# Feed-forward parts as units of one shape, with ScalarE and VectorE work written in a fixed order

## The chip, the cores and the metric

One Trainium2 chip; the program runs on one of its cores. The metric is the device time of the whole program in microseconds (us), the median of several executions. A TensorE matmul here takes a 128x128 block of weights and streams 128x256 or 128x512 features past it into a PSUM bank.

## The reference, cut to what matters

Two decoder layers, 512 tokens of 1024 features. Each layer runs a feed-forward half step, a token mixer (convolution and differential attention), and a second feed-forward half step:

```python
def swiglu(h, w_gate, w_up, w_down):
    return (jax.nn.silu(h @ w_gate) * (h @ w_up)) @ w_down

for l in range(DEPTH):
    x = x + 0.5 * swiglu(rms_norm(x, ffn1_norm[l]), ffn1_w_gate[l], ffn1_w_up[l], ffn1_w_down[l])
    h = rms_norm(x, mix_norm[l])
    ...                                             # the mixer
    x = x + jnp.concatenate([conv_out, diff_out], axis=-1) @ w_out[l]
    x = x + 0.5 * swiglu(rms_norm(x, ffn2_norm[l]), ffn2_w_gate[l], ffn2_w_up[l], ffn2_w_down[l])
```

The hidden width is 2816, which is 22 tiles of 128. Everything is float32. There are four feed-forwards in the program (two layers, two each); they are what the change touches.

## The kernel before, in words

**Numbers as pairs.** Weights and features are split into a high part (`whi`, `hh`, `acth`, `th`) and a low part (`wlo`, `hl`, `actl`, `tl`) that TensorE can multiply in its fast float32 form. A product is the sum of three matmuls: high by high, high by low, low by high. ScalarE makes the high part (a copy, `parts_of`, L100), VectorE the low part (raw minus high, L101).

**Parts.** `PARTS` (L45) cuts the 22 hidden tiles of a feed-forward into 5, 8 and 9. The first part of 5 is computed plainly. The parts of 8 and of 9 use a seven-product scheme (Winograd's form of Strassen's) in place of eight products of half blocks. A part first computes its hidden tiles, one gate and up tile at a time ("gate-up", `sums` L135 and `seven` L369), and then its share of the output projection in four steps, two output tiles a step ("down", `down_sums` L413 and `seven_down` L468). So the second part has 8 gate-up steps and 4 down steps, the third 9 and 4.

**One gate-up step.** `sums` loads the weights: the gate block g1,g2 (L145), then a tile with g1 and u2 (L147, L148), u2 once more (L150); then a DMA on GpSimd's queue adds u1 onto both halves of that second tile (L152, an accumulating transfer), which leaves g1+u1 and u2+u1. GpSimd adds up two more sums (L157, L158). `seven` issues the products in this order, 12 matmuls of 256 columns each: `u2u1` into c, `u2` into d, then (call of `before`, L393) the rest of the step ahead, its product `g1u1` into its own a; then `g1` into a, `g2` into b, `all` into c, `g1u2u1` into a. a and d are the halves of one PSUM bank, b and c of another. ScalarE saves intermediate sums in `keep` (L391, L395, L399), VectorE adds (L400) and ScalarE applies silu (L401). The rest: L404 to L408, then `Gated.add` (L540), which splits the hidden tile `us`, still in PSUM, into `hh` and `hl` (L549, L550).

**Pairs.** The first four hidden tiles of a part are paired for the down steps. An even one is saved in `hold` and differenced (L545, L546). After the odd one come the sums of the pair, straight on in `add` (L554 to L562); they end with `four`, made from the odd tile's `us` in PSUM on ScalarE (L561) and VectorE (L562).

**PSUM banks.** `pair_banks` (L325) gives each step two banks and goes around three such pairs. A step takes over the banks of the step three before it, and TensorE's first write waits until everything that reads the old contents is done.

**Weights in SBUF.** `ring` (L92) hands out buffers: five for raw weights (`wraw`), four each for high and low parts. A load waits until the old buffer has been read.

**What sets the order.** A scheduler with a model of the instructions' times orders each engine's queue when the program is built. `tc.keep_in_program_order` fixes one instruction behind the one traced before it on its engine. In the kernel before, only the first matmul of each product is fixed so; ScalarE, VectorE and GpSimd stand as the scheduler put them. Each engine then runs its queue strictly in order.

## Time and profile before

| | |
|---|---|
| median of 3 runs | 1799.3 us (1799.25 to 1803.62) |
| the profiled execution | 1802.17 us |
| its span, first to last instruction | 1800.2 us |
| TensorE granted clock | 0.999 |
| busy: VectorE, ScalarE, GpSimd | 1343.9, 977.6, 884.8 us |

The profile is one execution. PE is TensorE's matmuls, PEld its weight loads, DVE VectorE, ACT ScalarE, POOL GpSimd, SP the engine that issues most DMAs. `out<-in` names the program's tiles. A line such as L100 is a line of the kernel. An engine's idle time is put down to the instruction that released it.

### The profile page before, as it was taken

Reading aid. Unit: us, or ns where it says so; the run is one execution under the profiler, and the core shown is the slowest. Engines: PE = TensorE matmul, PEld = TensorE weight load, DVE = VectorE, ACT = ScalarE, POOL = GpSimd, SP = SyncE. Lnnn points to the kernel's source line nnn. Section 1 sums busy time; section 2 is a strip of 40 time slices with the busy share of each in tenths; the row PEclk is TensorE's granted clock in tenths of the full one; section 3 lists DMA queues with packets and bytes.
Section 4 is the critical chain, followed back from the end, with each engine's and each line's share of the span. In section 5 each row is a group of like instructions: output and inputs, shape, how many; then the busy total and the mean of one; then the engine's idle time right before and its main releaser. Section 6 shows DMA issues by size and latency. Waiting matters only on the chain. (4 is left out here: it accounts for less than half of the span.)

```text
span 1800.2 us, 30317 instructions
## 1 busy us (share of the span) xinstructions
PE 1776.3 (99%) x11437; PEld 1609.4 (89%) x11437; DVE 1343.9 (75%) x2021; ACT 977.6 (54%) x1691; POOL 884.8 (49%) x661
## 2 busy tenths in 40 slices
PE   9999999999999999999999999999999999999999
PEld 7899999888788899899888998998877888999998
DVE  7877687768857868687776776878688587786874
ACT  6465465545844456466543654655457454564652
POOL 2244545669952134444612354356699521345443
PEclk9999999999999999999999999999999999999999
DMA  7374565433122365565433645744331223655752
GB/s 245 109 186 123 146 180 148 139 107 94 47 71 82 94 164 130 141 181 151 127 118 98 165 117 156 185 135 154 93 99 43 71 94 88 167 145 146 181 148 71
DMA packets 112307, 231.36 MB, mean 129 GB/s; under 512 B 12215, under 2 KB 33990, under 8 KB 112160
## 3 DMA queue, kind: packets, MB, share of 16 engines
q1 hardware_dynamic: 92064, 191.93, 33.2%
q0 software_dynamic: 19808, 37.33, 12.2%
q8 instruction: 89, 1.46, 0.3%
q14 instruction: 58, 0.48, 0.1%
q10 hardware_dynamic: 288, 0.16, 0.0%
HBM read 227.26 MB, written 3.42 MB: 128 GB/s over the span
## 5 line engine op out<-in xcount | busy, mean ns | idle before, releaser
L100 ACT ACTIVATE whi<-wraw 128x512 fp32r<-128x512 f32 (+3 forms) x660 | 496.0, 777 | 498.1 <-PE ps_pair L386 135.5
L101 DVE TENSOR_TENSOR wlo<-wraw,whi 128x512 fp32r<-128x512 f32 (+2 forms) x617 | 602.7, 1000 | 179.2 <-ACT whi L100 174.2
L386 PE MATMUL ps_pair<-acth,wlo 128*128 128x256 f32 x1088 | 308.3, 283 | 1.9 <-DVE wlo L101 1.9
L386 PE MATMUL ps_pair<-actl,whi 128*128 128x256 f32 x1088 | 307.9, 283 | 0.0
L386 PE MATMUL ps_pair<-acth,whi 128*128 128x256 f32 x1088 | 307.8, 283 | 0.0
L157 POOL TENSOR_TENSOR wraw<-wraw 128x512 f32<-128x512 f32 x68 | 104.7, 1540 | 309.0 <-DMA wraw<-in_gu 205.5
L386 PE MATMUL ps_pair<-th,whi 128*128 128x256 f32 x816 | 231.7, 284 | 4.8 <-ACT keep L395 3.7
L386 PE MATMUL ps_pair<-th,wlo 128*128 128x256 f32 x816 | 230.9, 283 | 0.0
L386 PE MATMUL ps_pair<-tl,whi 128*128 128x256 f32 x816 | 230.9, 283 | 0.0
L152 POOL DMA_DIRECT2D wraw<-in_gu x68 | 82.0, 1206 | 268.2 <-DVE gs L617 111.9
L386 PEld LDWEIGHTS ps_pair<-acth,wlo 128*128 128x128 f32 x1088 | 208.8, 192 | 2.7 <-DVE wlo L101 2.7
L386 PEld LDWEIGHTS ps_pair<-actl,whi 128*128 128x128 f32 x1088 | 208.8, 192 | 0.3
L386 PEld LDWEIGHTS ps_pair<-acth,whi 128*128 128x128 f32 x1088 | 208.8, 192 | 0.3
L177 PE MATMUL ps_pair<-actl,whi 128*128 128x512 f32 x448 | 174.7, 391 | 0.6 <-DVE actl L263 0.6
L174 PE MATMUL ps_pair<-acth,whi 128*128 128x512 f32 x448 | 173.9, 392 | 0.8 <-ACT whi L100 0.7
L178 PE MATMUL ps_pair<-acth,wlo 128*128 128x512 f32 x448 | 174.2, 390 | 0.0
L386 PEld LDWEIGHTS ps_pair<-th,whi 128*128 128x128 f32 x816 | 156.6, 192 | 6.2 <-ACT keep L395 4.7
L386 PEld LDWEIGHTS ps_pair<-tl,whi 128*128 128x128 f32 x816 | 156.6, 192 | 0.0
L386 PEld LDWEIGHTS ps_pair<-th,wlo 128*128 128x128 f32 x816 | 156.6, 192 | 0.0
L101 POOL TENSOR_TENSOR wlo<-wraw,whi 128x1024 fp32r<-128x1024 f32 x44 | 105.5, 2402 | 37.3 <-ACT whi L100 37.3
L861 DVE SCALAR_TENSOR_TENSOR ps_y<-u,par,ps_y 128x512 f32<-128x512 f32 x156 | 117.6, 754 | 3.7
L158 POOL TENSOR_TENSOR wraw<-wraw 128x512 f32<-128x512 f32 x68 | 116.1, 1707 | 5.3
(214 smaller groups left out, 4177.5 us busy)
## 6 DMA issues: line engine op xcount, KB each, us to landing
wraw<-in_gu SPq DMA_DIRECT2D x208, 256.0 KB, 4.1
wraw<-in_gu SPq DMA_DIRECT2D x104, 512.0 KB, 3.7
wraw<-in_gu POOLq DMA_DIRECT2D x68, 512.0 KB, 5.6
wraw<-in_wqkv SPq DMA_DIRECT2D x24, 512.0 KB, 3.7
wraw<-in_wag SPq DMA_DIRECT2D x16, 512.0 KB, 3.6
wraw<-in_wout SPq DMA_DIRECT2D x16, 512.0 KB, 3.6
wraw<-in_dn SPq DMA_DIRECT2D x60, 128.0 KB, 3.3
wraw<-in_dn SPq DMA_DIRECT2D x20, 384.0 KB, 3.7
```

Source lines behind the costliest of these rows:

```text
L100: S.activation(hi, raw, AF.Copy)
L101: low = (eng or V).tensor_tensor(out=lo, in0=raw, in1=f32(hi), op=ALU.subtract)
L152: nc.gpsimd.dma_start(two.rearrange("p (b c) -> p b c", b=2), u[:, h[0]].unsqueeze(1).broadcast_to([P, 2, 512]), accum_op=ALU.add)
L157: G.tensor_tensor(more[:, h[0]], two[:, h[1]], whole[:, h[0]], op=ALU.add)
L158: G.tensor_tensor(more[:, h[1]], more[:, h[0]], whole[:, h[1]], op=ALU.add)
L174: first = T.matmul(ps, wh, xh, start=start, stop=False)
L177: T.matmul(ps, wh, xl, start=False, stop=False)
L178: T.matmul(ps, wl, xh, start=False, stop=stop)
L386: mm = T.matmul(ps, l, r, start=first and i == j == 0, stop=False, skip_group_check=True)
L861: V.scalar_tensor_tensor(ys[c] if t == PAD and not n else y, us[c][:, t : t + SEQ], pars[l][:, wc + t : wc + t + 1], y, op0=ALU.mult, op1= ...
```

## The change

`seven`, `down_sums` and `seven_down` become two classes, `GateUp` and `Down`, with one common `body`. The parts of 8 and 9 of a feed-forward become one list of 25 units (8 gate-up, 4 down, 9 gate-up, 4 down). The body of a unit issues its own products and, at fixed places between them, the splitting of the **next** unit's weights (`nxt.hi`, `nxt.lo`), the rest and finish of the unit ahead (`prev`), and the pair sums of the unit before that (`prev2.extras`). Every one of these ScalarE and VectorE instructions is now fixed in program order (`pinned`).

- Weights are grouped by when they are used: A holds u2u1 and u2, B holds g1 and g2, C holds g1u2u1 and all, D holds g1u1. The gate-up unit loads the tile that is added to first, then the gate block. The accumulating transfer and GpSimd's two sums stay.
- The pair sums move from `add`, one unit after the odd tile, to `combine`, called two units after it, behind the splitting of the next unit's A and D.
- In a down unit the two additions to `x` on GpSimd (L501, L510) go. VectorE adds the saved sums in PSUM and then adds to `x`: five VectorE instructions in place of three. For all but the first down unit of a part the plain products into the spare bank move ahead of the rest of the unit before.
- The product list, its order within a unit and the number of matmuls are the same.

The core of the diff (lines of the new kernel are named "new L..." below):

```diff
+    def pinned(ins, pin=PIN):
+        if pin:
+            tc.keep_in_program_order(ins)
+        return ins
...
+        def body(self, nxt, prev, prev2):
+            if nxt:
+                nxt.load()
+            self.begin()
+            self.go(self.c, "u2u1", "t1", first=True)
+            pinned(S.activation(self.keep[:, 3], self.c, AF.Copy))
+            if nxt and nxt.soon:
+                nxt.hi("A")
+                nxt.lo("A")
+            self.go(self.d, "u2", "t4", first=True)
+            self.early()
+            if nxt and self.early_free:
+                nxt.hi("B")
+            if prev:
+                prev.rest()
+            self.go(self.a, "g1", "b11")
+            pinned(S.activation(self.keep[:, :2], by_two(self.banks[0]), AF.Copy))
+            if prev:
+                prev.finish(0)
+            if nxt and self.early_free:
+                nxt.lo("B")
+            if prev:
+                prev.finish(1)
+            if nxt:
+                if not nxt.soon:
+                    nxt.hi("A")
+                    nxt.lo("A")
+                nxt.hi("D")
+                nxt.lo("D")
+            if prev:
+                prev.finish(2)
+            self.go(self.b, "g2", "b21")
+            self.middle()
+            if nxt:
+                nxt.hi("C")
+            if prev2:
+                prev2.extras()
+            self.go(self.c, "all", "b22")
+            self.go(self.a, "g1u2u1", "t2")
+            pinned(S.activation(self.keep[:, 2], self.a, AF.Copy))
+            self.close()
+            if nxt:
+                nxt.lo("C")
+                if not self.early_free:
+                    nxt.hi("B")
+                    nxt.lo("B")
...
+    class GateUp(Unit):
+        steps = KT // 2
+        soon = False
...
+        def load(self):
+            h = slice(0, 512), slice(512, 1024)
+            gate, up = self.src
+            two, g, u2 = ring("wraw"), ring("wraw"), ring("wraw2", 512)
+            nc.sync.dma_start(two[:, h[0]], gate[:, h[0]])
+            nc.sync.dma_start(two[:, h[1]], up[:, h[1]])
+            nc.sync.dma_start(g, gate)
+            nc.sync.dma_start(u2, up[:, h[1]])
+            nc.gpsimd.dma_start(
+                by_two(two), up[:, h[0]].unsqueeze(1).broadcast_to([P, 2, 512]), accum_op=ALU.add
+            )
+            more = ring("wraw")
+            G.tensor_tensor(more[:, h[0]], two[:, h[1]], g[:, h[0]], op=ALU.add)
+            G.tensor_tensor(more[:, h[1]], more[:, h[0]], g[:, h[1]], op=ALU.add)
+            self.raw = {"A": (two[:, h[1]], u2), "B": (g,), "C": (more,), "D": (two[:, h[0]],)}
...
+        def close(self):
+            g, two = self.keep[:, 0::2], by_two(self.banks[1])
+            pinned(V.tensor_tensor(two, two, g, op=ALU.add))
+            pinned(S.activation(g, two, AF.Silu))
+        def rest(self):
+            a, d, keep, us = self.a, self.d, self.keep, by_two(self.banks[0])
+            self.go(a, "g1u1", "t3")
+            pinned(V.tensor_tensor(d, a, keep[:, 3], op=ALU.add))
+            pinned(V.tensor_tensor(a, a, keep[:, 1], op=ALU.add))
+            pinned(V.scalar_tensor_tensor(us, us, -1.0, keep[:, 0::2], op0=ALU.mult, op1=ALU.mult))
+        def finish(self, n):
+            self.gated.add(self.n, self.banks[0], n)
+        def extras(self):
+            self.gated.combine(self.n, self.banks[0])
...
+    class Down(Unit):
...
+        def close(self):
+            A, B = 2 * self.q, 2 * self.q + 1
+            two, keep = by_two(self.banks[1]), self.keep
+            if not self.early_free:
+                self.plain(self.banks[1], 0)
+            pinned(V.tensor_tensor(two, two, keep[:, 0::2], op=ALU.add))
+            self.into(A, two, 0.5)
+            self.after(A)
+            if not self.early_free:
+                self.spare()
+            two = by_two(self.ps)
+            pinned(V.tensor_tensor(two, two, keep[:, 1::2], op=ALU.subtract))
+            self.into(B, two, 0.5)
...
+        def add(self, n, us, step):
+            a, b = slice(0, HS), slice(HS, SEQ)
+            first = self.paired(n) and n % 2 == 0
+            if step == 0:
+                if first:
+                    self.held[n] = self.fp.tile([P, SEQ], F32, tag=("hh8", "hl8")[n // 2 % 2], name="hold")
+                    pinned(S.activation(self.held[n], us, AF.Copy))
+                else:
+                    self.part_hi(n, us)
+            if step == 1:
+                if first:
+                    pinned(V.tensor_tensor(us[:, b], self.held[n][:, a], self.held[n][:, b], op=ALU.subtract))
+                    self.part_hi(n, us)
+                else:
+                    self.part_lo(us)
+            if step == 2 and first:
+                self.part_lo(us)
...
+        def combine(self, n, us):
+            if not self.paired(n) or n % 2 == 0:
                 return
-            t = self.hold
...
+            a, b = slice(0, HS), slice(HS, SEQ)
+            t = self.held[n - 1]
+            pinned(V.tensor_tensor(t[:, b], us[:, b], t[:, b], op=ALU.subtract))
+            pinned(V.scalar_tensor_tensor(t[:, a], t[:, a], -1.0, t[:, b], op0=ALU.mult, op1=ALU.subtract))
+            pinned(V.scalar_tensor_tensor(us[:, a], us[:, a], -1.0, t[:, a], op0=ALU.mult, op1=ALU.subtract))
             hi, lo, four = (self.part(tag) for tag in self.STORE[n // 2])
...
+            pinned(S.activation(hi, t, AF.Copy))
+            pinned(S.activation(four[:, a], us[:, a], AF.Copy))
+            pinned(V.tensor_tensor(lo, t, f32(hi), op=ALU.subtract))
+            pinned(V.tensor_tensor(four[:, b], us[:, a], f32(four[:, a]), op=ALU.subtract))
             self.sums.append((hi, lo, four))
```

In the new kernel's lines, the five pair sums on VectorE are new L668, L669, L670, L674 and L675, the two on ScalarE new L672 and L673; the three adds of the rest are new L511 to L513; the two matmul lines of the units are one, new L377.

## The prediction

> **What bounds the kernel now.** I read the page first, then the chain that ended last, then what TensorE waited for.

> ```profile
> span 1800.2 us, 30317 instructions
> ...
> PE 1776.3 (99%) x11437; PEld 1609.4 (89%) x11437; DVE 1343.9 (75%) x2021; ACT 977.6 (54%) x1691; POOL 884.8 (49%) x661
> ```

> ```profile
> 1660.75 86.43 PE ps_pair L386 x720
> ...
> 1775.98 3.43 PE ps_pair L491 x15
> ...
> 1795.46 0.70 DVE x L516
> ...
> 1796.29 0.69 DVE x L520
> ```

> In the last feed-forward 720 matmuls of 256 columns follow each other in 86.43 us, 0.120 us each; one of 512 columns takes 3.43/15 = 0.229. TensorE is the bound, and the change leaves every matmul in place. So it can only win back what TensorE waits. These are the waits of its weight loads that belong to the changed lines:

> ```profile
> PEld ps_pair L386 <- ACT keep L395: 4.7, 5, 1.4
> PEld ps_pair L491 <- DVE hl L550: 3.1, 4, 0.9
> PEld ps_pair L482 <- ACT keep L496: 3.0, 6, 1.0
> PEld ps_pair L386 <- DVE wlo L101: 2.7, 4, 1.2
> ...
> PEld ps_pair L491 <- ACT hh L549: 2.2, 1, 2.2
> ...
> PEld ps_pair L386 <- ACT keep L399: 1.3, 1, 1.3
> ```

> Together 4.7 + 3.1 + 3.0 + 2.7 + 2.2 + 1.3 = **17.0 us**: the most that can be gained, about 0.9%. Everything else that the change shortens or lengthens counts only if TensorE comes to wait for it.

> **The change, part by part.** A gate-up unit is 84 matmuls, 10.08 us; I count from its first matmul. Products take 1.44 us each: u2u1 from 0, u2 from 1.44, the rest of the unit ahead from 2.88 to 4.32, then g1, g2, all, and g1u2u1 to 10.08. Units are named by their hidden tile, 0 to 7 or 8.

> *The waits that go: -17.0.* In the new order the save of a and d (new L406) stands first in ScalarE's queue once TensorE has made them, at 5.96, 2.7 us ahead of its use; c's save is always at the unit's beginning; the last tile's hh and hl, by the sums below, are some 0.6 us early for the plain products. I take all 17.0 as gained, and half of it as the lower end.

> *The pair sums: the new wait.* They move behind the next unit's weights, and they are the last readers of a PSUM bank. In the changed program's queue the first matmul of `u2` in the units of tiles 4 and 6 waits for new L675, the last sum of the pairs 0,1 and 2,3, because those units take over the banks of tiles 1 and 3. All eight parts have both. Before, the same sums stood here (VectorE in the unit of tile 3, third part of the first feed-forward; TensorE's row is the u2 product of tile 4):

> ```profile
> 240.12 0.43 DVE L405 TENSOR_TENSOR ps_pair<-ps_pair,keep 128x256 f32<-128x256 f32 x1
> 240.59 0.43 DVE L406 TENSOR_TENSOR ps_pair<-ps_pair,keep 128x256 f32<-128x256 f32 x1
> 241.18 1.23 DVE L101 TENSOR_TENSOR wlo<-wraw,whi 128x1024 fp32r<-128x1024 f32 x1 [0.15 <-ACT whi L100]
> 242.32 0.69 DVE L408 SCALAR_TENSOR_TENSOR ps_pair<-ps_pair,keep 128x512 f32<-128x512 f32 x1
> ...
> 245.87 0.68 DVE L550 TENSOR_TENSOR hl<-ps_pair,hh 128x512 fp32r<-128x512 f32 x1
> 246.47 0.41 DVE L555 TENSOR_TENSOR hold<-ps_pair,hold 128x256 f32<-128x256 f32 x1
> 246.91 0.42 DVE L556 SCALAR_TENSOR_TENSOR hold<-hold 128x256 f32<-128x256 f32 x1
> 247.25 0.68 DVE L101 TENSOR_TENSOR wlo<-wraw,whi 128x512 fp32r<-128x512 f32 x1
> 247.85 0.42 DVE L557 SCALAR_TENSOR_TENSOR ps_pair<-ps_pair,hold 128x256 f32<-128x256 f32 x1
> 248.19 0.68 DVE L101 TENSOR_TENSOR wlo<-wraw,whi 128x512 fp32r<-128x512 f32 x1
> 248.78 0.69 DVE L400 TENSOR_TENSOR ps_pair<-ps_pair,keep 128x512 f32<-128x512 f32 x1
> 249.39 0.68 DVE L560 TENSOR_TENSOR hs<-hold,hs 128x512 fp32r<-128x512 f32 x1
> 249.99 0.42 DVE L562 TENSOR_TENSOR hs<-ps_pair,hs 128x256 fp32r<-128x256 f32 x1
> ```

> ```profile
> 257.20 0.28 PE L386 MATMUL ps_pair<-th,whi 128*128 128x256 f32 x1
> ```

> L562 ends at 250.41, and u2 starts at 257.20: 6.8 us to spare. The starts also give the pace: a queue of 512-wide instructions advances 0.60 each, a dependent 256-wide one 0.45. ScalarE's paces:

> ```profile
> 236.43 0.60 ACT L549 ACTIVATE hh<-ps_pair 128x512 fp32r<-128x512 f32 x1 [1.48 <-DVE ps_pair L546]
> 236.93 1.14 ACT L100 ACTIVATE whi<-wraw 128x512 fp32r<-128x512 f32 x2
> 237.97 0.37 ACT L399 ACTIVATE keep<-ps_pair 128x256 f32<-128x256 f32 x1
> ```

> Now VectorE's new queue in the unit of tile 3. The rest of tile 2 ends at 4.32, its last matmul drains 0.16 later. L511 4.52, L512 4.99, L513 5.46 to 6.14; low part of B to 7.29; the difference for tile 2 (new L646) to 7.63. ScalarE needs that for hh, 0.60 to 8.25, and only then splits A: first half done 8.79. VectorE: A 8.80 to 10.08, D to 10.68, hl to 11.28, then L668 to 11.60, L669 to 12.06, L670 to 12.52. ScalarE's copy L672 (0.63) ends at 12.71, L673 at 13.05; L674 runs 12.73 to 13.41, **L675 ends at 13.8**. TensorE wants that bank at 10.08 + 1.44 = 11.52: it waits **2.3 us**. Behind the waiting matmul stands all of TensorE's queue, so this is time of the kernel.

> In the unit of tile 5 no even tile is finished: A's split starts at 7.2, D ends at 9.7, L670 at 10.9, L674 at 11.83, L675 at 12.2: a wait of **0.7 us**.

> GpSimd can lengthen this. Median and longest of L560 (now L674), and GpSimd's pace:

> ```profile
> L560 DVE TENSOR_TENSOR hs<-hold,hs x16: 681/684/1802, 122.5 to 1709.6; 128x512 fp32r<-128x512 f32 x16
> ```

> ```profile
> 259.08 0.43 SPq L148 DMA_DIRECT2D wraw<-in_gu  x1
> ```

> ```profile
> 254.56 1.19 POOL L152 DMA_DIRECT2D wraw<-in_gu  x1
> 260.52 1.28 POOL L157 TENSOR_TENSOR wraw<-wraw 128x512 f32<-128x512 f32 x1 [4.77 <-DMA wraw<-in_gu]
> 261.88 2.17 POOL L158 TENSOR_TENSOR wraw<-wraw 128x512 f32<-128x512 f32 x1
> 264.56 1.20 POOL L152 DMA_DIRECT2D wraw<-in_gu  x1 [0.51 <-DMA wraw<-in_gu]
> ```

> The buffer for the tile that is added to, two tiles on, comes free with the low part of D, at 9.7 in the unit of tile 2. From there: some 0.8 to issue both pieces, 264.56 - 259.08 = 5.5 until the accumulating transfer can be issued, 260.52 - 254.56 = 6.0 until GpSimd's first sum: 9.7 + 12.3 = 22.0, or 11.9 in the unit of tile 3. So the two sums (3.5 us) cover 11.9 to 15.4, where L674 stands. I take the long L674 there, 1.1 more: 3.4. In the unit of tile 5 L674 starts before the sums: 0.7. Ends: without any lengthening 2.3 + 0.7; with L669 held up too and L674 long at tile 5 as well, 4.0 + 1.8. Eight parts: **8 x (3.4 + 0.7) = +32.8**, between 24.0 and 46.4.

> [...]

> *keep behind the sums.* The save of a (new L429) stands behind L672 and L673 and ends at about 13.4; the rest that needs it would start at 12.96. The bank wait covers it; without that, it costs 0.4 a part.

> *Ends of a feed-forward: +4.2.* TensorE's last row:

> ```profile
> 1795.85 0.28 PE L482 MATMUL ps_pair<-hs,wlo 128*128 128x256 f32 x1
> ```

> The last down unit's rest now follows directly on the product whose sum ScalarE must save first (0.16 + 0.37 + latency): 0.6 at three of four ends; at the other, matmuls of the next stage stand between. At the kernel's end five VectorE instructions follow the save, 0.62 to 4.0, while the last matmul drains at 1.5: 2.5 behind it, against 0.85 before (L520 ends at 1796.29 + 0.69 = 1796.98, the last matmul at 1795.85 + 0.28 = 1796.13): +1.6. Ahead of a mixer the same lateness reaches the statistics: I take 0.4 twice.

> *What lies beside other work.*

> ```profile
> L501 POOL TENSOR_TENSOR x<-x,keep 128x512 f32<-128x512 f32 x32 | 52.3, 1633 | 18.9 <-ACT keep L500 18.8
> ```

> GpSimd loses its 64 additions to x; VectorE gets 64 of 0.69, 44 us in the down units. There it has about 7.2 us of work (five of 0.69, and four low parts) in 10.5 or 11.9: hidden. One split in six fewer per gate-up unit also lies off the path. The accumulating loads are due at about 7.2 in the unit after that where they land at 1.8: 5 us to spare, so load order costs nothing.

> Sum: -17.0 + 32.8 + 4.2 = **+20.0**. Against the profiled execution's 1802.2 that is 1822; that execution lies 2.9 above the median of the runs, so against 1799.3: **1819.3**. This forecast alone spans 1808 to 1834.

> **The rivals.**
> - *Faster.* The fixed order removes the 17.0 and the bank comes free in time: 1799.3 - 17.0 + 4.2 = 1786.5. It decides at 7.2 us from the end of tile 2's rest (4.32) to L675; I count 9.5. For it: 6.8 us to spare before. Against it: ScalarE's and VectorE's steps in that stretch stand in one chain. [...] 0.10.
> - *No change.* Both waits together come to 1.6 a part, if VectorE starts the sums earlier than I count: 12.8 - 17.0 + 4.2 = 0, so 1799.3. 0.08.
> - *The order fits no better:* as many waits appear at other places as go: 1799.3 + 32.8 + 4.2 = 1836. Fixed queues with splits that wait on loads speak for it, the spare times above against. 0.12.
> - *The accumulating transfers set the pace:* if they land over 5 us later than in the rows above, every gate-up unit grows; at 0.5 us for each of 68, 34 more: 1853. 0.05.

> **How the numbers follow.** The forecast has 0.65. The range 1800 to 1838 leaves out the first, the last and about half of the second rival. A measurement of this kernel tells about 0.3% (5.4 us) from no change. Faster: 0.11; within: 0.08; slower: 0.81.

> **What would show it.** Right: TensorE waits for VectorE new L675 16 times, 2.3 to 4 us at tile 4 and 0.7 to 1.8 at tile 6 of each part, some 33 us in all; the old six waits are gone; VectorE's sums stand behind the low part of D; GpSimd's sums lie over L674. Wrong: no wait on L675, or waits on high and low parts of weights, or GpSimd's idle time before L472 growing in each unit.

## The result and the profile after

The changed kernel is slower: median 1856.2 us of 4 runs (1852.93 to 1859.08) against 1801.5 of 4 runs of the kernel before on the same chip; ratio 1.0303, 95% interval 1.0276 to 1.0329. The forecast was 1819.3, in a range of 1800 to 1838: the sign was right, the size was not. The profiled execution took 1854.8 us.

The page and the row of the core, after (span; busy time and share of each engine; the core's span and mean granted clock of TensorE):

```profile
span 1852.9 us, 30039 instructions
...
PE 1791.8 (97%) x11437; PEld 1621.6 (88%) x11437; DVE 1333.2 (72%) x2017; ACT 951.8 (51%) x1623; POOL 756.5 (41%) x597
```

```profile
core 0: 1852.9 us, clock 0.989
```

TensorE has the same 11437 matmuls. Its busy share fell from 99% to 97%, and its clock from 0.999 to 0.989. So two things are to be found: where it waits, and why its clock is lower. What TensorE waited for, after (total, times, longest):

```profile
PE ps_pair L377 <- DVE hs L675: 31.6, 16, 3.5
PE ps_d L138 <- ACT hh L628: 8.9, 3, 7.1
PE ps_pair L377 <- ACT keep L429: 3.2, 3, 1.4
PE ps_pair L377 <- ACT keep L406: 2.4, 2, 1.2
```

None of the six waits that the prediction added up to 17.0 us is left at its place; ScalarE's saves are waited for at the ends of a feed-forward alone (L406, L429). In their place stand 16 waits for the last pair sum, as forecast, and three rows that are not in the sum, or in it with another size.

**The pair sums.** VectorE in the unit of tile 3, third part of the first feed-forward (start, duration), GpSimd's two weight sums beside it, then TensorE at the first u2 product of tile 4:

```profile
265.89 0.69 DVE L491 TENSOR_TENSOR wlo<-wraw,whi 128x512 fp32r<-128x512 f32 x1
266.49 0.69 DVE L661 TENSOR_TENSOR hl<-ps_pair,hh 128x512 fp32r<-128x512 f32 x1
267.09 0.42 DVE L668 TENSOR_TENSOR hold<-ps_pair,hold 128x256 f32<-128x256 f32 x1
267.54 1.33 DVE L669 SCALAR_TENSOR_TENSOR hold<-hold 128x256 f32<-128x256 f32 x1
268.91 0.43 DVE L670 SCALAR_TENSOR_TENSOR ps_pair<-ps_pair,hold 128x256 f32<-128x256 f32 x1
269.57 0.98 DVE L674 TENSOR_TENSOR hs<-hold,hs 128x512 fp32r<-128x512 f32 x1 [0.23 <-ACT hs L672]
270.47 0.41 DVE L675 TENSOR_TENSOR hs<-ps_pair,hs 128x256 fp32r<-128x256 f32 x1
```

```profile
267.34 1.25 POOL L472 TENSOR_TENSOR wraw<-wraw 128x512 f32<-128x512 f32 x1 [4.48 <-DMA wraw<-in_gu]
268.67 1.33 POOL L473 TENSOR_TENSOR wraw<-wraw 128x512 f32<-128x512 f32 x1
```

```profile
270.94 0.39 PE L377 MATMUL ps_pair<-th,whi 128*128 128x256 f32 x1 [3.46 <-DVE hs L675]
...
272.20 0.42 PE L377 MATMUL ps_pair<-th,whi 128*128 128x256 f32 x1
272.42 0.42 PE L377 MATMUL ps_pair<-tl,whi 128*128 128x256 f32 x1
```

The chain is the forecast's: the low part of D (L491), hl, then the sums, and TensorE starts when L675 has ended. From the starts of the matmuls, the eight stalls at tile 4 are 2.74 to 3.61 us, at tile 6 0.80 to 1.91; in all 34.2 us beyond the normal pace, where the sum had 32.8. The last rows show something else: 1.3 us after TensorE resumes, matmuls of 256 columns start every 0.22 us instead of every 0.12. The windows of one microsecond around it (the first number after the five engines' counts is the granted clock):

```profile
268.00:269.00 1.00, 0.00 (x0) 0.00 (x0) 0.97 (x2) 0.09 (x1) 0.92 (x2) 1.00 0.76 213
...
272.00:273.00 1.00, 1.00 (x7) 1.00 (x6) 0.61 (x1) 1.00 (x3) 0.34 (x1) 0.50 0.00 0
273.00:274.00 1.00, 1.00 (x7) 1.00 (x6) 0.00 (x0) 0.34 (x1) 0.00 (x0) 0.50 0.84 121
274.00:275.00 1.00, 1.00 (x7) 1.00 (x7) 0.00 (x0) 0.00 (x0) 0.00 (x0) 0.50 1.21 197
275.00:276.00 1.00, 1.00 (x8) 1.00 (x8) 0.39 (x1) 0.00 (x0) 0.00 (x0) 0.80 0.92 154
```

For 3.4 us the clock is 0.50, and by the starts of the matmuls this costs 1.5 us. Over the span the clock is under 1 in nine stretches. TensorE stood idle in parts of them; what the matmuls in them lost adds up, by their starts, to 14.5 us, against 1.6 in the kernel before. Each stretch lies in or behind a gap of TensorE's. So a stall of 3 us can cost 3 + 1.5.

**The plain part.** ScalarE in the first feed-forward, then TensorE:

```profile
53.52 1.36 ACT L715 ACTIVATE gs<-gs 128x512 f32<-128x512 f32 x2
69.97 0.63 ACT L487 ACTIVATE whi<-wraw 128x512 fp32r<-128x512 f32 x1 [15.08 <-DMA wraw<-in_gu]
70.50 1.04 ACT L101 ACTIVATE whi<-wraw 128x1024 fp32r<-128x1024 f32 x1
71.45 0.61 ACT L628 ACTIVATE hh<-gs 128x512 fp32r<-128x512 f32 x1
```

```profile
72.11 1.22 PE L138 MATMUL ps_d<-hh,whi 128*128 128x512 f32 x2 [7.13 <-ACT hh L628]
```

L487 is the split of group D of the first of the 25 units, which come *after* the plain part. The change leaves the splits of `units[0]` to the scheduler, which put this one ahead of work that was ready. ScalarE sits 15.1 us in front of it until the accumulating transfer has landed; the plain part's hh is behind it in the queue, though it could have run: in e13 below, where this split stands later, ScalarE makes the same hh at 58.66. With two smaller places TensorE loses 9.6 us.

**The ends.** ScalarE at the end of a feed-forward that a mixer follows:

```profile
368.51 1.06 ACT L101 ACTIVATE whi<-wraw 128x1024 fp32r<-128x1024 f32 x1 [4.37 <-issue]
369.48 0.71 ACT L226 ACTIVATE acth<-x,par 128x512 fp32r<-128x512 f32 x1
370.09 0.61 ACT L235 ACTIVATE sq<-x 128x512 f32<-128x512 f32 x1
370.61 0.58 ACT L406 ACTIVATE keep<-ps_pair 128x512 f32<-128x512 f32 x1
```

The save L406 stands behind what `after` puts on ScalarE for the mixer. TensorE loses 1.36 us for it and 1.51 for L429 just after, at two ends, and 0.63 for L429 at the kernel's end: 6.4 us.

The spans differ by 52.7 us. To add up the parts, the six old waits have to be counted like the new ones, by the starts of the matmuls: so counted they come to 15.2 us. The 17.0 is idle time of the weight loads, part of which lies beside running matmuls. The sum: -15.2 + 34.2 + 9.6 + 6.4 + (14.5 - 1.6) = 47.9. Of the rest 1.7 lies at the kernel's end, where the span now goes on for 6.0 us after the start of the last matmul in place of 4.3, and some 3 in the mixers.

### The profile page after: what moved, and what is told of

It is laid out like the page before. It is cut to its first block, busy times and chain, and to the rows that moved or that the text cites. A ratio compares the mean times of both kernels' runs of the same rounds, so it can differ in the third digit from the quotient of the medians.

```text
span 1852.9 us, 30039 instructions
## 1 busy us (share of the span) xinstructions
PE 1791.8 (97%) x11437; PEld 1621.6 (88%) x11437; DVE 1333.2 (72%) x2017; ACT 951.8 (51%) x1623; POOL 756.5 (41%) x597
## 5 line engine op out<-in xcount | busy, mean ns | idle before, releaser
L491 DVE TENSOR_TENSOR wlo<-wraw,whi 128x512 fp32r<-128x512 f32 (+1 forms) x340 | 325.6, 989 | 59.2 <-ACT whi L487 59.0
L377 PE MATMUL ps_pair<-acth,whi 128*128 128x256 f32 x1088 | 308.4, 283 | 0.0
L377 PE MATMUL ps_pair<-actl,whi 128*128 128x256 f32 x1088 | 308.2, 283 | 0.0
L377 PE MATMUL ps_pair<-acth,wlo 128*128 128x256 f32 x1088 | 308.0, 283 | 0.0
L487 ACT ACTIVATE whi<-wraw 128x512 fp32r<-128x512 f32 (+1 forms) x340 | 251.0, 799 | 54.0 <-DMA wraw<-in_gu 30.4
L377 PE MATMUL ps_pair<-th,whi 128*128 128x256 f32 x816 | 235.6, 289 | 31.6 <-DVE hs L675 31.6
L472 POOL TENSOR_TENSOR wraw<-wraw 128x512 f32<-128x512 f32 x68 | 95.1, 1398 | 390.9 <-DMA wraw<-in_gu 246.0
L377 PE MATMUL ps_pair<-th,wlo 128*128 128x256 f32 x816 | 234.2, 287 | 0.0
L377 PE MATMUL ps_pair<-tl,whi 128*128 128x256 f32 x816 | 234.1, 287 | 0.0
L377 PEld LDWEIGHTS ps_pair<-acth,whi 128*128 128x128 f32 x1088 | 209.4, 192 | 0.2
L377 PEld LDWEIGHTS ps_pair<-actl,whi 128*128 128x128 f32 x1088 | 209.2, 192 | 0.2
L377 PEld LDWEIGHTS ps_pair<-acth,wlo 128*128 128x128 f32 x1088 | 209.1, 192 | 0.0
L101 ACT ACTIVATE whi<-wraw 128x1024 fp32r<-128x1024 f32 (+3 forms) x124 | 122.6, 999 | 143.3 <-PE ps_pair L141 83.3
L377 PEld LDWEIGHTS ps_pair<-th,whi 128*128 128x128 f32 x816 | 159.3, 195 | 34.9 <-DVE hs L675 34.9
L138 PE MATMUL ps_pair<-acth,whi 128*128 128x512 f32 x448 | 174.0, 395 | 0.3 <-ACT whi L101 0.2
L406 ACT ACTIVATE keep<-ps_pair 128x512 f32<-128x512 f32 x100 | 59.6, 596 | 197.3 <-PE ps_pair L377 197.3
L377 PEld LDWEIGHTS ps_pair<-th,wlo 128*128 128x128 f32 x816 | 159.8, 196 | 0.0
L377 PEld LDWEIGHTS ps_pair<-tl,whi 128*128 128x128 f32 x816 | 159.6, 196 | 0.0
L367 DVE TENSOR_TENSOR wlo<-wraw,whi 128x1024 fp32r<-128x1024 f32 (+2 forms) x128 | 123.6, 990 | 16.5 <-ACT whi L363 16.4
```

What stands on the lines that cost most here:

```text
L101: S.activation(hi, raw, AF.Copy)
L138: first = T.matmul(ps, wh, xh, start=start, stop=False)
L367: pinned(V.tensor_tensor(out=lo[:, :c], in0=self.raw[k][:, :c], in1=f32(hi[:, :c]), op=ALU.subtract), pin)
L377: mm = T.matmul(ps, l, r, start=first and i == n == 0, stop=False, skip_group_check=True)
L406: pinned(S.activation(self.keep[:, :2], by_two(self.banks[0]), AF.Copy))
L472: G.tensor_tensor(more[:, h[0]], two[:, h[1]], g[:, h[0]], op=ALU.add)
```

## The experiments

Theory 1: the place of the pair sums in VectorE's queue costs most of it, with half clock behind the stalls. Theory 2: the first unit's split in front of the plain part. Theory 3: the ends. Rivals: the fixed order as such, or the accumulating transfers. All ratios are to the kernel before on the same chip:

| kernel | median us | ratio, 95% interval |
|---|---|---|
| the change | 1856.2 | 1.0303 (1.0276 to 1.0329) |
| e1 sums early | 1818.0 | 1.0110 (1.0084 to 1.0136) |
| e2 first unit fixed | 1853.5 | 1.0306 (1.0279 to 1.0333) |
| e3 = e1 + e2 | 1812.2 | 1.0073 (1.0051 to 1.0096) |
| e4 no fixed order | 1809.6 | 1.0061 (1.0039 to 1.0083) |
| e5 = e3 + ends | 1805.5 | 1.0033 (1.0020 to 1.0046) |
| e6 = e5, D last | 1824.8 | 1.0134 (1.0120 to 1.0149) |
| e7 low D behind sums | 1842.0 | 1.0231 (1.0212 to 1.0251) |
| e8 idle matmuls | 1847.6 | 1.0266 (1.0251 to 1.0281) |
| e9 = e5, first D late, spare cut | 1817.1 | 1.0081 (1.0060 to 1.0103) |
| e10 = e9, B first | 1816.0 | 1.0073 (1.0052 to 1.0094) |
| e11 = e2, first D late | 1853.9 | 1.0285 (1.0260 to 1.0309) |
| e12 = e5, only D fixed | 1801.3 | 0.9998 (0.9983 to 1.0013) |
| e13 = change, only D fixed | 1843.1 | 1.0230 (1.0207 to 1.0253) |

**e1: the sums early.**

```diff
             pinned(S.activation(self.keep[:, 3], self.c, AF.Copy))
+            if prev2:
+                prev2.extras()
...
                 nxt.hi("C")
-            if prev2:
-                prev2.extras()
```

> The changed kernel with one call moved: the pair sums of the tile before last (L668 to L675) stand right behind the copy of c into the keep tile (L395), ahead of the additions of the unit before (L511 to L513), no longer behind the next unit's splits. Theory 1 (place of the pair sums in VectorE's queue): the 16 waits of ps_pair L377 for hs L675 (31.6 us by the chain of waits, 34.2 us by the pitch of the matmuls) go, and with them the about 8 us of matmuls at a longer pitch right behind them; 1856 becomes 1810 to 1824. Rival A (the fixed order itself holds VectorE back): what is taken out in one place comes back as waits for L511 to L513 or for keep L406 in the same units, time above 1840. Rival B (accumulating transfers set the pace): no change, 1850 to 1860. If the longer pitch has nothing to do with the stalls, 1822 and the pitch stays.

From 1.0303 to 1.0110: about 35 us came back with one moved call. The waits that take their place are small:

```profile
PE ps_d L138 <- ACT hh L628: 9.6, 4, 7.4
PE ps_pair L377 <- DVE wlo L491: 4.0, 8, 1.3
PE ps_pair L377 <- ACT keep L429: 3.2, 3, 1.4
```

No row for L675 is left, so VectorE had the time earlier in the unit. Rivals A and B fall. The gain is at the weak end of the range, since 4.0 us for low parts and 2.4 for high parts (at the unit behind the sums) are new: VectorE is nearly full in these units (busy for 0.86 of 805 to 816 us in this trace, a stretch with the sums in it).

**e2: the first unit's splits fixed too.**

```diff
-                units[0].hi(k, False)
-                units[0].lo(k, False)
+                units[0].hi(k)
+                units[0].lo(k)
```

> The changed kernel with only the splits of the first unit of each feed-forward part sequence put under the fixed order as well (the two False arguments at units[0] taken away). On ScalarE that moves one copy in each of four places: the 128x512 split of g1u1 (whi from wraw), which stood ahead of the plain part's hh copy and sat up to 15.1 us for its transfer. Theory 2: the wait of ps_d L138 for hh L628 (8.9 us in 3) goes and with it the matmuls at half pace behind it; 1856 becomes 1843 to 1847. Rival: the plain part is held by its own transfers, or the first unit is now late by the same time; 1852 to 1858. The pair sums' waits (31.6 us in 16) stay in both.

A miss: the wait for hh went and the time stayed. TensorE's waits, and VectorE ahead of the first unit's product:

```profile
PE ps_pair L377 <- DVE hs L675: 30.7, 16, 3.7
PE ps_pair L377 <- DVE wlo L491: 5.0, 6, 1.1
```

```profile
90.58 0.69 DVE L734 SCALAR_TENSOR_TENSOR x<-ps_d,x 128x512 f32<-128x512 f32 x1 [2.25 <-PE ps_d L142]
91.19 2.42 DVE L491 TENSOR_TENSOR wlo<-wraw,whi 128x512 fp32r<-128x512 f32 x3
```

Fixing all four groups put A, which the first product needs, behind the plain part's last addition to x (L734), which needs TensorE's last plain matmul. TensorE waits 1.31 us beyond its pace at the first unit of each of the four feed-forwards, 5.2 us, and 2.4 more in four waits two units on. By the starts of the matmuls 7.7 of the 9.6 us are given back, and the 2 that are left are less than the interval of the ratio. So the rival holds, the first unit is now late. That leaves Theory 2 open; e13 moves group D alone.

**e3: both.**

> Both edits: the pair sums right behind the copy of c, and the first unit's splits under the fixed order. If the two losses are separate places on one path the gains add: 42 + 12 us off 1856, so 1797 to 1808; what is left against the kernel before (1801) is then the ends of the feed-forward (about 6 us more) against the old waits that went (17 us). Rival: the two share an aftermath or another engine closes the gap: above 1815.

1812, at 1.0073: beyond the forecast 1797 to 1808. Both halves give less than was priced: the sums 35 in place of 42 (e1), and the first unit some 7 over e1 in place of 12.

**e4: no fixed order** (`PIN = False`).

> The changed kernel with the switch of the fixed order off: units, their one shape, the additions on VectorE and the accumulating transfers stay, but the scheduler orders ScalarE and VectorE. If the loss is where the fixed order puts the pair sums (Theory 1), the scheduler issues them when they are ready and most of the 16 waits go: 1800 to 1822. If the loss is the units' shape or the transfers whatever the order, 1840 to 1860.

1.0061. With units, their shape, additions on VectorE and accumulating transfers all kept, 44 us of the 55 are gone when the scheduler places the instructions. The scheduler's L675 costs no wait. Of what is left its waits show

```profile
PE ps_d L138 <- ACT hh L628: 8.9, 3, 7.1
PE ps_d L138 <- DVE x L734: 4.6, 3, 2.1
PE ps_pair L377 <- ACT keep L429: 3.2, 3, 1.4
```

**e7: a smaller dose.** Only VectorE's part of group D moves behind the sums.

```diff
                 nxt.hi("D")
-                nxt.lo("D")
...
             if prev2:
                 prev2.extras()
+            if nxt:
+                nxt.lo("D")
```

> The changed kernel with one split moved: VectorE's part of group D (one 128x512, about 0.6 us) stands behind the pair sums, no longer ahead of them. A dose test of Theory 1: if each bank wait is the length of VectorE's queue ahead of L675, every one of the 16 shrinks by that 0.6 us, about 9.5 us in all (31.6 to 22), and half a window or more of half clock with it; 1856 becomes 1842 to 1848. Rival (the waits are set by ScalarE's copies L672 and L673 or by the wait for L641, not by the queue): the 16 waits stay at 30 to 32 us and the time at 1853 to 1858.

```profile
PE ps_pair L377 <- DVE hs L676: 19.3, 10, 2.8
```

(L675 and L676 here are L674 and L675 of the change.) The waits shrink by 12.3 us, more than 9.5, and the time by some 13 (ratio 1.0303 to 1.0231). At tile 4 the stalls are 0.62 us shorter in the mean, about the length of the split that moved. At tile 6 they shrink by 0.89, as the sum ahead of the last one also runs undisturbed there more often (it takes over 1 us in one of eight, in the change in five); six of the eight fall under what counts as a wait. So the wait is the length of VectorE's queue ahead of the last sum, with what GpSimd adds to it.

**e8: TensorE kept busy in the stall.** Ahead of u2 in the unit of tile 4:

```diff
+        def fill(self):
+            if self.n == 4:
+                ps = bank("tp", "ps_idle")
+                for _ in range(10):
+                    mm = T.matmul(ps, ones_r, ones_r.unsqueeze(1).broadcast_to([P, NT, P]), start=True, stop=True)
+                    tc.keep_in_program_order(mm)
```

> The changed kernel with ten matmuls on constants (128x512, 2.27 us at full pace, into a bank of their own that nothing reads) put ahead of the first u2 matmul of tile 4, where TensorE stands 2.7 to 3.6 us for hs L675. They take nothing out of the wait for L675, but TensorE no longer idles through it. If the half clock (0.50 for 3.4 us) behind these waits comes from TensorE's standing idle, four of the windows in the trace of the changed kernel (at 271, 831, 1186 and 1746 us) go, 1.7 us each: 1856 becomes 1847 to 1851. If it comes from something else (power, transfers), they stay: 1854 to 1859.

Eight times 2.27 us of work on constants is added, and the kernel is some 7 us faster. The intervals of the two ratios touch, but the mean clocks of the runs do not: 0.993 to 0.995 in four runs, 0.987 to 0.990 in four of the change. The wait for the last sum (L686 here) is as long, only filled: 18.2 us are matmuls on constants and 14.1 stay idle, most of it at tile 6, which gets no filling. The waits and the clock:

```profile
PE ps_pair L377 <- DVE hs L686: 14.1, 16, 1.6
```

```profile
core 0: 1846.5 us, clock 0.995
```

No half clock is left behind the stalls at tile 4, where there were four, nor at tile 6, where there was one; what is left lies at the other places (plain part, attention, an end ahead of a mixer, the kernel's end), in part shorter. Transfers and pair sums are as before, so the half clock comes from TensorE's standing idle. The filling was worth about 7 us.

**e5: the ends.** The call of `after` for the second tile moves behind the saves; the last unit's plain product runs between g1u2u1 and g1u1.

```diff
+            if prev:
+                prev.done()
+            if self.last:
+                self.spare()
             self.close()
...
             self.into(B, self.a.unsqueeze(1).broadcast_to([P, 2, HS]), -0.5)
-            self.after(B)
+        def done(self):
+            self.after(2 * self.q + 1)
```

> The kernel of e3 with the end of each feed-forward rearranged: the call of after for the second tile of the unit before stands behind the copies of the keep tile, no longer ahead of them on ScalarE, and the last unit's plain product of its second tile (ps_d) runs between g1u2u1 and g1u1, where TensorE waited for keep L429. Theory 3: the waits for keep L408 (2.4 us in 2) and keep L429 (3.2 us in 3) go, and with them the two windows of half clock (1.7 us each) that stand right behind them in the trace of e3; 1812 becomes 1802 to 1806. Rival: the mixer's first work, for which the call prepares, is late by as much; 1810 to 1813.

From 1.0073 to 1.0033, about 7 us, as Theory 3 has it. The waits for the saves L406 (L408 in e3) and L429 are gone; 3.7 us in 3 for c's save (L395) took their place, and the half clock at the ends went.

**e6: D last.**

> The kernel of e5 with the next unit's g1u1 split (group D, needed last) put behind all other work of the unit on both engines, so that VectorE has the pair sums of two units and the splits that are needed at the next unit's start off its queue sooner. In e3 TensorE still waits 6.6 us in 13 for wlo L491 at the start of units; if VectorE's queue is what makes these late, they go: 1797 to 1801. Rival: they wait for the transfers or for ScalarE's halves, no change, 1802 to 1806.

A miss of the sign: 1.0134, some 18 us slower than e5. The waits for low parts grew (9.0 in 22, from 6.6 in 13), those for high parts to 5.2 in 10 (from 1.3 in 2) and those for L395 to 5.2 in 3 (from 3.7); 4.1 us in 3 for the low parts of the down weights came up. By the starts of the matmuls these make 15 of the 17 us between the two spans.

**e9 and e10.** In e9 the first unit's group D goes behind the second's A, and the last unit's plain product is cut in two; e10 moves the sums behind ScalarE's copy of B.

> The kernel of e5 with two more edits: the first unit's g1u1 split (group D, first needed by the second unit) stands behind the second unit's group A on ScalarE and VectorE, since in e5 TensorE waits 1.31 us for wlo at the second unit of each of the four part sequences (5.2 us); and the last unit's plain product is cut, two tiles early and three between g1u2u1 and g1u1, since in e5 TensorE waits 3.7 us in 3 for keep L395 there. If these waits stand on the path: 1805 becomes 1795 to 1799, level with the kernel before or a little under it (1800). Rival (VectorE's queue is full and the waits come up a unit later): 1802 to 1805.

> The kernel of e9 with the pair sums behind ScalarE's copy of group B, so that L672 and L673, which wait for VectorE, no longer hold that copy back. If ScalarE's queue makes the 0.3 to 0.4 us waits for wlo and whi at tiles 4 and 6 (about 4 us in all in e5): 2 to 4 us under e9. Rival: VectorE is the fuller one there, no change within 1 us.

Both miss: e9 is some 9 us slower than e5, e10 like e9 within the intervals. I had misread the place: the 1.31 us stand at the first unit, not the second (see e2). GpSimd's first weight sums behind 100 us, in e5 and then in e9:

```profile
104.17 1.28 POOL L480 TENSOR_TENSOR wraw<-wraw 128x512 f32<-128x512 f32 x1 [4.48 <-issue]
105.53 1.28 POOL L481 TENSOR_TENSOR wraw<-wraw 128x512 f32<-128x512 f32 x1
```

```profile
108.83 1.29 POOL L483 TENSOR_TENSOR wraw<-wraw 128x512 f32<-128x512 f32 x1 [8.27 <-DMA wraw<-in_gu]
110.19 1.63 POOL L484 TENSOR_TENSOR wraw<-wraw 128x512 f32<-128x512 f32 x1
```

Groups A and D are halves of one raw tile. Holding D's split back keeps that tile, and GpSimd's weight sums come 4.7 us later. ScalarE waits for them, and TensorE 9.2 us in 5 for ScalarE's high parts. The same may be behind e6's loss; no run shows that. The cut plain product did take away the 3.7 us for L395, and 4.5 us for the mixer's statistics (ps_rows, waiting for ssum) appeared.

**e11: e2 with the first unit's D late.**

> The changed kernel with the first unit's splits under the fixed order, as in e2, and with that unit's group D behind the second unit's group A. In e2 the wait of ps_d L138 for hh L628 (8.9 us) went and the time stayed, with 5.0 us of new waits for wlo L491, four of 1.31 us at the second units. If what e2 took away came back as these waits and as half-clock windows at other places: now 5 us less than e2 by the waits, 1845 to 1850. Rival (the plain part's stall was hidden by something else that ends as late): 1852 to 1857, as e2.

1.0285: like e2, and the four waits at the first units are still there, for the same misreading.

**e12 and e13: only group D fixed.**

```diff
-                units[0].hi(k, False)
-                units[0].lo(k, False)
+                units[0].hi(k, k == "D")
+                units[0].lo(k, k == "D")
```

> The changed kernel with only group D of the first unit's splits under the fixed order; A, B and C stay with the scheduler. If the wait of ps_d L138 for hh L628 (8.9 us in 3 by the chain of waits, and two windows of half clock behind it) stands on the path by itself: 1856 becomes 1843 to 1848, with no wait for wlo L491 in its place. Rival (what this stall takes is given back at the next waits for L675 whatever the splits' order): 1852 to 1857.

> The kernel of e5 (pair sums early, ends rearranged) with only group D of the first unit's splits under the fixed order and A, B and C left to the scheduler, as in the changed kernel. If the four waits of 1.31 us for wlo at the first units come from A standing behind the plain part's additions to x (L734 of the changed kernel), they go: 1805 becomes 1798 to 1802, level with the kernel before. Rival (VectorE is late there whatever the order): 1804 to 1807.

Both come out as forecast. In e13 the waits for hh are gone, the two longest rows are the change's others, and nothing stands in for hh:

```profile
PE ps_pair L377 <- DVE hs L675: 31.0, 16, 3.6
PE ps_pair L377 <- ACT keep L429: 3.2, 3, 1.4
```

and the ratio falls from 1.0303 to 1.0230, 13 us: Theory 2 holds after all; e2 had given the gain back at the first units. In e12, with the sums early and the ends mended, the kernel is level with the one before. Its span is 1798.6 us, its clock 1.000, TensorE is busy 99% again, and its longest rows of waits are:

```profile
PE ps_pair L377 <- DVE wlo L499: 3.8, 8, 1.3
PE ps_pair L377 <- ACT keep L395: 3.7, 3, 1.3
```

In parts of the time before, the sums cost 1.93% (e1), the split 0.73% (e13) and the ends 0.40% (e5 against e3), together 3.06% of 3.03%. Each of these differences is uncertain by some 0.3 to 0.4 points, so the close fit is in part luck; the better proof is e12, which mends all three at once and is level. What each mending costs is in these figures too. By the starts of the matmuls the 15.2 us of old waits are gone in e12 as well, but 11.5 us of new ones for low parts, high parts and c's save stand in their place: the change without its three faults gains nothing that can be measured.

## Why the prediction was wrong

Two terms that the sum puts at nothing are the steps that failed: what the clock does after a stall, and a split that waits for a transfer ahead of ready work.

- *TensorE bounds, and only its waits count:* TensorE does bound, but this step failed in its price: a wait was counted at its length, with nothing for the matmuls behind it. The half clock cost some 13 us net (14.5 against 1.6), and e8 shows that it follows from the standing idle. A row that shows it stood in the trace of before, behind gaps of TensorE's in an attention stage:

```profile
503.00:504.00 1.00, 1.00 (x7) 0.90 (x6) 1.00 (x6) 0.98 (x4) 0.96 (x1) 0.50 0.00 0
504.00:505.00 1.00, 1.00 (x5) 0.81 (x4) 1.00 (x5) 0.93 (x4) 0.13 (x1) 0.50 0.00 0
```

  The mean over the span, 0.999, hides it.
- *What lies beside other work:* this is the second step that failed. "Load order costs nothing" looked at the accumulating loads of units in steady state and not at `units[0]`, whose splits stay with the scheduler. A split that waits for a transfer stood ahead of hh of the plain part, 9.6 us by the starts of the matmuls. Alone it is worth 13 us of the time (e13).
- *The waits that go, -17.0:* right in that none of the six is left, too large by 1.8 (15.2 by the starts of the matmuls). What the saves still cost stands at the ends and is counted there.
- *The pair sums, +32.8:* right in place, chain and count. That the size came out too (34.2) is partly luck: by tile it was 3.4 and 0.7, and the mean was 3.0 and 1.3, two errors that nearly cancel. Both lie in sums that were longer while GpSimd's two weight sums ran. At tile 4 GpSimd's came earlier than forecast: over the eight parts L669, beside them each time, took 0.46 to 1.33 us, 0.71 in the mean, in place of 0.42, and L674 0.98 in place of 0.69, together 0.6 and not the 1.1 of L674 alone. At tile 6 L674 took 1.03 to 1.80 in the five of eight where it lay beside them for 0.95 us or more, and 0.69 in the other three, where the sum has it undisturbed throughout. L668 and L670 kept to 0.42 and 0.43 beside GpSimd's sums too. The 4.0 at tile 4, in the upper end of the sum, has L669 held up as well; no row of before shows that (there the same sum, L556, took 424 to 426 ns and never ran beside GpSimd's). In the changed kernel L669 was held up, and still no part reached 4.0 (longest 3.6).
- *Ends, +4.2:* at the kernel's end it was right: 0.63 for L429 (forecast 0.6), and 1.7 later behind the last matmul (forecast 1.6). At the two ends ahead of a mixer the mechanism of L429 was right and the size not, 1.51 instead of 0.6, and that L406 stands behind what `after` puts on ScalarE (1.36 twice) was not seen. e5 prices all ends at 7 us, half clock included.
- *The rivals:* "the order fits no better", at 1836, was nearest in mechanism. It named splits that wait on loads, and one such split did cost; but the wait came from an instruction that was not fixed. The rival of the accumulating transfers, at 1853, is nearest in number by chance: they did not set the pace, since e1 and e12 keep them.
- *The range:* its upper end, 1838, took in the sums' long case, but no term for what follows a stall. (With the half of 17.0 that the prediction names as the lower end it would have been 1841.) With 12.9 for the clock, 9.6 for the plain part, 3.9 more at the ends and 15.2 in place of 17.0 the sum would have been 1847.5.

## What to carry to other kernels

When instructions are put in a fixed order, list for every PSUM bank its last reader and put that reader ahead of work that is not yet due; here one call's place was worth 35 us. Read also the instructions that were left out of the fixed order: one of them that waits for a transfer holds everything behind it on its engine, here ScalarE for 15.1 us. And price a stall of TensorE at its length plus what the clock may lose after it, here up to 1.5 us for a stall of 3.

## What the runs showed of the hardware

```profile
1209.12 0.39 PE L377 MATMUL ps_pair<-th,whi 128*128 128x256 f32 x1 [1.75 <-DVE hs L675]
```

```profile
1211.00:1212.00 1.00, 1.00 (x7) 1.00 (x6) 0.00 (x0) 0.53 (x1) 0.96 (x1) 0.50 0.25 25
```

- The length of a stall alone does not tell which is followed by it. At tile 4, in us beyond the normal pace, the four with half clock behind them are 2.86, 2.88, 3.00 and 3.61 long, the four without it 2.74, 2.75, 3.00 and 3.09.
- Ten matmuls on constants in a stall that has to be waited out anyway keep the clock up (mean 0.993 to 0.995 instead of 0.987 to 0.990) and save some 7 us (e8).
